# VectorE instead of GpSimd for the affine part of the residual and for the low weight parts at a layer's end

## The chip, the cores and the metric

The kernel runs on one core of a Trainium2 chip. The metric is the device time of one execution in microseconds (us). A core has a matrix engine (TensorE, PE in the profile; PEld is its weight load), VectorE (DVE), ScalarE (ACT), GpSimd (POOL) and SyncE (SP), whose queue issues the DMA transfers here. Each engine takes its instructions in the order in which the program lists them; engines wait for each other through semaphores.

## The reference, cut to what matters

One transformer block over 256 tokens of width 2048, in float32: a gated feed-forward network, a mixer (differential attention beside a gated delta rule) and a second feed-forward network. Each ends with a residual and a layer norm, and scale, shift and gate come from a vector `c`:

```python
ada = (jax.nn.silu(c) @ w_ada[l] + b_ada[l]).reshape(B, N_SUB, 3, D_MODEL)
shift, scale, gate = ada[:, :, 0, None], ada[:, :, 1, None], ada[:, :, 2, None]
y = swiglu_ffn(x * (1.0 + scale[:, 0]) + shift[:, 0], w_ffn_in[l, 0], w_ffn_out[l, 0])
x = layer_norm(DEEPNORM_ALPHA * x + 0.5 * gate[:, 0] * y, ln_g[l, 0], ln_b[l, 0])
y = hybrid_mixer(x * (1.0 + scale[:, 1]) + shift[:, 1], ...)
x = layer_norm(DEEPNORM_ALPHA * x + gate[:, 1] * y, ln_g[l, 1], ln_b[l, 1])
y = swiglu_ffn(x * (1.0 + scale[:, 2]) + shift[:, 2], w_ffn_in[l, 1], w_ffn_out[l, 1])
x = layer_norm(DEEPNORM_ALPHA * x + 0.5 * gate[:, 2] * y, ln_g[l, 2], ln_b[l, 2])
```

`layer_norm` multiplies the normed row by `ln_g` and adds `ln_b`: the affine part.

## The kernel before

**Products in three parts.** Every float32 matrix is split into a high part `hi` (a rounded copy) and a low part `lo` (what is left), and a product is three matmuls: high by high, low by high, high by low. A weight chunk of 128x1024 goes through four hands: SyncE loads it into one of six `raw` buffers, ScalarE writes `hi`, another engine subtracts and writes `lo` (four buffers each), and TensorE uses both in 24 matmuls of 256 columns or 12 of 512. A raw buffer is loaded anew when its `lo` is done; a `hi` buffer is written anew when TensorE is through with it. Which engine writes `lo` is decided in `_split`:

```python
eng = self.P if self.pool_lo and i % self.pool_lo == 0 else self.V
eng.tensor_tensor(lo, raw, hi.bitcast(F32), ALU.subtract)
```

`k.V`, `k.A` and `k.P` stand for VectorE, ScalarE and GpSimd. `pool_lo` is 1 or 2 in parts of the first layer's beginning, and 1 again at the ends of the first two layers, from `_Next.step` at stage 0 to `_Next.rest`.

**The order.** The kernel is written as Python generators ("threads") that a small planner steps while it writes TensorE's program. `k.t` is planned time; a thread that yields 8.0 is taken up again 8 planned us later, and what it then issues is put at that place of its engine's queue. So the planned times fix the order of each queue, and the chip decides the real times.

**The gate vectors.** `_Ada` loads `w_gate` chunks (`ar`, two buffers) and lets VectorE add them up: two instructions per chunk into `acc` (128x512), eight chunks for each quarter of a gate. Then ScalarE and VectorE split `acc` into `acchi` and `acclo`, and two matmuls with a matrix of ones (`aps`) sum over partitions. They stand in TensorE's queue between weight matmuls.

**The residual.** A layer's input after its norm is stored without the affine part (`xd`). `_load_x` reads it back while the next layer computes: into two tiles `x` (one per 128 tokens), then for each quarter of 512 columns the rows `ln_g` and `ln_b`, spread over 128 partitions, into `rowg` and `rowb` (one buffer each), and `x = x * rowg + rowb` for both tiles: 16 instructions in a layer, on GpSimd. This happens in the second layer (the mixer, while its output gates are multiplied, `gth`, `mf`, `mgl`) and in the third (the second feed-forward network, while `hid` is computed). The result is needed by the layer's output blocks, later.

**The layer end.** `_y_blocks` computes four output blocks of 512 columns; the last is cut into halves (`tail`), so that residual (`res`, `x`), statistics (`st`, `mv`, `rs`) and norm of one half run beside the matmuls of the next. Meanwhile weights of the next layer are loaded and split. TensorE then transposes the normed rows (`lnt`) and starts the next layer (`pre`).

Of the kernel before, what the change touches and what calls it, by code (L numbers as in the profile page):

```python
# [12 lines left out]
ALU = mybir.AluOpType  # L13
# [43 lines left out]
class _Thread:  # L57
# [6 lines left out]
    def step(self):  # L64
        k = self.k
        k.chain = k.t
        try:
            lat = next(self.gen)
            self.ready = k.t + max(0.0, lat) if lat is not None else k.t + MARGIN * (k.chain - k.t) + 0.3
        except StopIteration:  # L70
            self.done = True
            k.threads.remove(self)
# [186 lines left out]
def _products(k, ps, w, kt0, nkt, acts, first, last):  # L259

    nb = len(acts)
    hv, lv = [x.rearrange("p (k b m) -> p k b m", k=nkt, b=nb) for x in w]
    for j in range(nkt):
        for b in range(nb):
            acts[b].need(k, kt0 + j)
            ah, al = acts[b]
            k.mm3(ps[:, b, :], (hv[:, j, b, :], lv[:, j, b, :]),
                  (ah[:, kt0 + j, :], al[:, kt0 + j, :]),
                  start=(first and j == 0 and b == 0),
                  stop=(last and j == nkt - 1))  # L270
            k.pump()
# [214 lines left out]
def _new_h(k):  # L486
    u = k.uid()
    h = _H([k.pp.tile([128, KT, S], F32R, tag=f"h_{x}", name=f"h_{x}{u}") for x in ("hi", "lo")])
    h.ready = 0
    return h  # L490


def _h_tile(k, pool, h, f, src, A, B):

    nc = k.nc
    hf = pool.tile([128, S], F32, tag="hf", name=f"hf{k.uid()}", bufs=3)
    k.V.tensor_scalar(hf, src, A, B, ALU.mult, ALU.add)
    k.A.activation(h[0][:, f, :], hf, AF.Copy)
    k.P.tensor_tensor(h[1][:, f, :], hf, h[0][:, f, :].bitcast(F32), ALU.subtract)
# [45 lines left out]
class _Next:  # L545
# [5 lines left out]
    def step(self, stage, ada, ln):  # L551
        k = self.k
        if stage == 0:
            k.pool_lo = 1
            self.A = None
        elif stage == 1:
            ln.root(0)
        elif stage == 2:
            ln.factors(0)
        else:  # L560
            ln.norm(0, 0)
            ln.norm(0, 1)
            ln.root(1)
            return self.rest(ln)
        if self.A is None and (ada.thread.done or stage == 2):
            k.wait(lambda: ada.thread.done)
            self.A, self.B = self.prep(ada)

    def rest(self, ln):
        k, A, B = self.k, self.A, self.B  # L570
        h = _new_h(k)
        x, lnp = k.x, k.lnp
        k.xd = k.drp.tile([128, 2, D], F32, tag="xd", name=f"xd{self.idx}")

        def turn(ps, g, t):
            for j in range(2):
                f = 2 * g + j
                k.tr(ps[:, j, t * 128:(t + 1) * 128], x[t][:, f * 128:(f + 1) * 128])

        def bank(g):  # L580
            ps = k.pss.tile([128, 2, 256], F32, tag="sm", name=f"lnt{k.uid()}")
            turn(ps, g, 0)
            return ps

        ln.norm(0, 2)
        ln.norm(0, 3)
        pss = [bank(g) for g in range(3)]
        ln.factors(1)
        ln.norm(1, 0)
        k.pool_lo = 0  # L590
        def run():
            for g in range(8):
                ps = pss.pop(0)
                turn(ps, g, 1)
                for i in range(2):
                    f = 2 * g + i
                    _h_tile(k, lnp, h, f, ps[:, i, :], A[:, f:f + 1], B[:, f:f + 1])
                if g in (0, 2, 4):
                    ln.norm(1, 1 + g // 2)
                h.ready = 2 * g + 2  # L600
                h.when[2 * g] = h.when[2 * g + 1] = k.chain
                yield 0.0
                if g < 5:
                    pss.append(bank(g + 3))
            for t in range(2):
                k.nc.sync.dma_start(k.xd[:, t, :], x[t])

        th = k.spawn(run())
        th.step()
        acts = [h, h]  # L610
        pre = [k.bank([128, 2, S], "pre") for _ in range(2)]
        for c in range(4):
            for ps in pre:
                _products(k, ps, k.weights(), 4 * c, 4, acts, c == 0, c == 3)
        k.wait(lambda: th.done)
        return h, pre
# [46 lines left out]
def _load_x(k, a, pool, rows, tags, idx, delay, pace):  # L663

    nc = k.nc
    k.x = None
    yield delay
    x = [pool.tile([128, D], F32, tag=tags[t], name=f"x{k.uid()}") for t in range(2)]
    for q in range(4):
        for t in range(2):  # L670
            sl = slice(q * 512, (q + 1) * 512)
            nc.sync.dma_start(x[t][:, sl], k.xd[:, t, sl])
            k.load()
        yield pace
    for q in range(4 if idx is not None else 0):
        sl = slice(q * 512, (q + 1) * 512)
        g, b = [rows.tile([128, 512], F32, tag=n, name=f"{n}{k.uid()}", bufs=1) for n in ("rowg", "rowb")]
        nc.sync.dma_start(g, a["ln_g"][idx:idx + 1, sl].to_broadcast([128, 512]))
        nc.sync.dma_start(b, a["ln_b"][idx:idx + 1, sl].to_broadcast([128, 512]))
        yield 8.0  # L680
        for t in range(2):
            k.P.tensor_tensor(x[t][:, sl], x[t][:, sl], g, ALU.mult)
            k.P.tensor_tensor(x[t][:, sl], x[t][:, sl], b, ALU.add)
    k.x = x


# [73 lines left out]
def _ffn(k, a, h, sub, items, interval, start, pre, finish, tail):  # L760
# [4 lines left out]
    with ExitStack() as fs:  # L765
        k.hp = hp = fs.enter_context(tc.tile_pool(name=f"hid{sub}", bufs=1))
        for half, size in enumerate(SIZES[sub]):
            hid = _H([{}, {}])
            hid.ready = size
            j0 = 0  # L770
            if half == 0:

                def side():
                    k.pss = k.pss or k.ctx.enter_context(tc.tile_pool(name="pss", bufs=4, space=PSUM))
                    ada = _Ada(k, a, fs.enter_context(tc.tile_pool(name=f"ada{sub}", bufs=1)), items, interval)
                    k.lnp = fs.enter_context(tc.tile_pool(name=f"ln{sub}", bufs=1))
                    k.spawn(_load_x(k, a, k.lnp, k.lnp, ("x0", "x1"), *((1, 40.0, X_PACE) if sub else (None, 0.0, 3.0))))
                    return ada

                if start is not None:  # L780
                    j0 = size
                    ada = start(h, hid, side)
                    k.spawn(_rel_bias(k, a))
                    k.spawn(_lambda(k, a))
                    k.spawn(k.consts())
                else:
                    j0 = len(pre)
                    for j in range(j0):
                        _ffn_hid(k, pre[j], hid, j, back=j0 - j)
                    ada = side()  # L790
            for j in range(j0, size):
                ps = _wstat(k, 4, acts)
                _ffn_hid(k, ps, hid, j)
            res = _y_blocks(k, size // 2, hid, ada, sub, half == 0, ln if half else None, finish, tail)
# [103 lines left out]
def _delta_pair(k, g, kq2, v2, nz, yb, before, stage):  # L898
# [166 lines left out]
    for h in range(2):  # L1065
        k.mm(pz[:, reg(h)], U[:, 2 * h, 0, :], vn[:, 2 * h, :])
    z = tl("z", (128, 2, 128))
    k.A.activation(z, rest(pz[:, 0:256]), AF.Copy)
    yield

# [6 lines left out]
    for h in range(2):  # L1077
        k.mm(pS[:, reg(2 + h)], NQ[:, 2 * h, 1, :], z[:, h, :])
    St = tl("St", (128, 2, 128))
    k.V.tensor_copy(St, rest(pS[:, 0:256]))  # L1080
    for h in range(2):
        out(2 * h, pS[:, reg(2 + h)])
    oNv = oN.rearrange("p (h t) j -> p h t j", t=2)
    k.V.tensor_copy(oNv[:, :, 0, :], rest(pS[:, 256:512]))
    stage[0] = 4 * g + 2
    yield
# [619 lines left out]
```

## Time and profile before

| what | value |
|---|---|
| median of 3 runs | 2416.9 us (2414.76 to 2419.35) |
| the profiled execution's own time | 2417.43 us |
| its span, first to last instruction | 2415.6 us |
| outside the span | 1.8 us |
| mean granted TensorE clock | 0.984 of 2.4 GHz |
| PE busy | 2331.5 us (97%) |
| DVE busy | 1708.3 us (71%) |
| ACT busy | 1036.6 us (43%) |
| POOL busy | 323.1 us (13%) |

All times inside the execution count from the span's start. The layers end near 800 us and near 1637 us. A timeline row gives start, duration, engine, line, operation, output and inputs; "x2" merges two like instructions that follow each other, and the bracket names the idle time before it and what ended it.

### The profile page before, as it was taken

To read this page: it belongs to the slowest core of one execution; us is meant where nothing else is said; L and a number is where in the kernel's file an instruction comes from. 1 tells how busy PE (TensorE), PEld (TensorE's weight loads), DVE (VectorE), ACT (ScalarE), POOL (GpSimd) and SP (SyncE) were. 2 spreads that over 40 slices of the span, in tenths; PEclk is the share of its full clock that TensorE was granted. 3 is DMA by queue.
4 is the path that set the end of the run, shared out by engine and by line. 5 is a ranking of instruction groups with operands and counts; after the bars stand their busy time and mean duration, and the time that the engine had idled before them with its cause. 6 is when DMAs were issued, how large, how long until landed. Compare 5 with 4: busy or idle time off the path is not lost.

```text
span 2415.6 us, 42349 instructions
## 1 busy us (share of the span) xinstructions
PE 2331.5 (97%) x16989; PEld 2214.6 (92%) x16989; DVE 1708.3 (71%) x2538; ACT 1036.6 (43%) x1420; POOL 323.1 (13%) x218
## 2 busy tenths in 40 slices
PE   6999999999999899999999999999999999999997
PEld 6999997889998879998999999988999989999987
DVE  4767888787765687869887887876787555444456
ACT  4434444444444444444444344435434434444432
POOL 5884000000002210000000300022040000000001
PEclk8999999999999999999999999999999999999999
DMA  9997878898875565544547888876888555555553
GB/s 363 333 329 289 296 248 275 317 336 301 300 262 191 183 206 193 168 166 153 168 160 262 299 308 291 290 261 214 300 311 261 188 192 192 183 183 183 186 191 106
DMA packets 166381, 582.06 MB, mean 241 GB/s; under 512 B 19820, under 2 KB 22812, under 8 KB 165416
## 3 DMA queue, kind: packets, MB, share of 16 engines
q1 hardware_dynamic: 166184, 579.36, 68.9%
q8 instruction: 133, 2.18, 0.4%
q14 instruction: 64, 0.52, 0.1%
HBM read 572.98 MB, written 7.88 MB: 240 GB/s over the span
## 4 chain that ended last, share of the span: by engine, by line
PE 87%; DVE 7%; issue 2%; ACT 1%; DMA 1%; POOL 1%; DVEq 0%; SPq 0%; ACTq 0%; POOLq 0%
PE mm L147 15%; PE mm L148 15%; PE mm L149 15%; PE mx L149 8%; PE mx L147 8%; PE mx L148 8%; PE mms L148 4%; PE mms L147 4%; PE mms L149 4%; DVE lo L88 2%; DVE acc L88 1%; PE UY L153 1%; DVE x L88 1%; ACT hi L88 1%; PE pre L148 1%
## 5 line engine op out<-in xcount | busy, mean ns | idle before, releaser
L88 ACT ACTIVATE hi<-raw 128x1024 fp32r<-128x1024 f32 x769 | 811.9, 1059 | 995.9 <-PE mm L148 413.4
L88 DVE TENSOR_TENSOR lo<-raw,hi 128x1024 fp32r<-128x1024 f32 x690 | 855.2, 1245 | 524.6 <-ACT hi L88 516.8
L147 PE MATMUL mm<-h_hi,hi 128*128 128x256 f32 x3072 | 878.1, 286 | 0.0
L149 PE MATMUL mm<-h_hi,lo 128*128 128x256 f32 x3072 | 868.0, 283 | 3.6 <-DVE lo L88 3.6
L148 PE MATMUL mm<-h_lo,hi 128*128 128x256 f32 x3072 | 869.6, 283 | 0.0
L149 PEld LDWEIGHTS mm<-h_hi,lo 128*128 128x128 f32 x3072 | 583.3, 190 | 4.3 <-DVE lo L88 4.3
L147 PEld LDWEIGHTS mm<-h_hi,hi 128*128 128x128 f32 x3072 | 581.6, 189 | 1.9 <-issue 1.6
L148 PEld LDWEIGHTS mm<-h_lo,hi 128*128 128x128 f32 x3072 | 581.6, 189 | 1.0 <-issue 0.6
L88 POOL TENSOR_TENSOR lo<-raw,hi 128x1024 fp32r<-128x1024 f32 x79 | 189.9, 2412 | 793.4 <-ACT hi L88 793.4
L147 PE MATMUL mx<-hi,hid 128*128 128x512 f32 (+1 forms) x772 | 285.3, 370 | 1.4 <-ACT hi L88 1.4
L148 PE MATMUL mx<-lo,hid 128*128 128x512 f32 (+1 forms) x772 | 285.3, 370 | 0.8 <-DVE lo L88 0.8
L149 PE MATMUL mx<-hi,hid 128*128 128x512 f32 (+1 forms) x772 | 285.1, 369 | 0.0
L147 PE MATMUL mms<-h_hi,hi 128*128 128x256 f32 x896 | 256.2, 286 | 9.9 <-ACT hi L88 5.7
L148 PE MATMUL mms<-h_lo,hi 128*128 128x256 f32 x896 | 255.4, 285 | 3.7 <-POOL h_lo L88 3.7
L149 PE MATMUL mms<-h_hi,lo 128*128 128x256 f32 x896 | 254.3, 284 | 1.6 <-POOL lo L88 1.6
L147 PEld LDWEIGHTS mms<-h_hi,hi 128*128 128x128 f32 x896 | 170.5, 190 | 10.6 <-ACT hi L88 5.8
L148 PEld LDWEIGHTS mms<-h_lo,hi 128*128 128x128 f32 x896 | 171.3, 191 | 4.3 <-POOL h_lo L88 4.2
L149 PEld LDWEIGHTS mms<-h_hi,lo 128*128 128x128 f32 x896 | 172.1, 192 | 1.9 <-POOL lo L88 1.9
L147 PEld LDWEIGHTS mx<-hi,hid 128*128 128x128 f32 x772 | 145.5, 189 | 26.7 <-ACT hi L88 1.9
L148 PEld LDWEIGHTS mx<-lo,hid 128*128 128x128 f32 x772 | 145.5, 188 | 25.9 <-DVE lo L88 1.4
L149 PEld LDWEIGHTS mx<-hi,hid 128*128 128x128 f32 x772 | 145.5, 188 | 24.4
L88 DVE SCALAR_TENSOR_TENSOR acc<-ar,cs,acc 128x512 f32<-128x512 f32 x180 | 147.7, 821 | 6.3 <-DMA ar<-in_w_gate_dram 2.9
(295 smaller groups left out, 2436.7 us busy)
## 6 DMA issues: line engine op xcount, KB each, us to landing
raw<-in_w_ffn_in_dram SPq DMA_DIRECT2D x240, 512.0 KB, 4.4
raw<-in_w_ffn_out_dram SPq DMA_DIRECT2D x176, 512.0 KB, 4.1
raw<-in_w_first_dram SPq DMA_DIRECT2D x112, 512.0 KB, 5.1
ar<-in_w_gate_dram SPq DMA_DIRECT2D x96, 512.0 KB, 4.9
ar<-in_w_ada_dram SPq DMA_DIRECT2D x96, 512.0 KB, 5.4
sar<-in_w_ada_dram SPq DMA_DIRECT2D x64, 512.0 KB, 4.7
raw<-in_w_gab_dram SPq DMA_DIRECT2D x64, 512.0 KB, 4.7
raw<-in_w_kq_dram SPq DMA_DIRECT2D x32, 512.0 KB, 3.2
```

What stands on the lines that cost most here:

```text
L88: return f(*args, **kw)
L147: mm(ps, lhsT=lhs[0], rhs=rhs[0], start=start, stop=False, skip_group_check=True)
L148: mm(ps, lhsT=lhs[0], rhs=rhs[1], start=False, stop=False, skip_group_check=True)
L149: mm(ps, lhsT=lhs[1], rhs=rhs[0], start=False, stop=stop, skip_group_check=True)
L153: self.nc.tensor.matmul(ps, lhsT=lhsT, rhs=rhs, start=start, stop=stop, skip_group_check=True)
```

## The change

`pool_lo` is no longer set at the layers' ends, so the seven low parts of each end are VectorE's. The 32 affine instructions are VectorE's too, and each has its own step: a quarter was one wait of 8 planned us and four instructions at once; now it is 4 planned us and then four instructions with 2 planned us ahead of each, 12 in all.

```diff
     def step(self, stage, ada, ln):
         k = self.k
         if stage == 0:
-            k.pool_lo = 1
             self.A = None
...
         ln.factors(1)
         ln.norm(1, 0)
-        k.pool_lo = 0
+
         def run():
...
-        yield 8.0
+        yield 4.0
         for t in range(2):
-            k.P.tensor_tensor(x[t][:, sl], x[t][:, sl], g, ALU.mult)
-            k.P.tensor_tensor(x[t][:, sl], x[t][:, sl], b, ALU.add)
+            for v, op in ((g, ALU.mult), (b, ALU.add)):
+                yield 2.0
+                k.V.tensor_tensor(x[t][:, sl], x[t][:, sl], v, op)
```

The first place is SyncE's queue in the mixer, where the second quarter's rows are loaded. `raw` is a weight load, `ar` a load of the gate's weights, and the bracket names the semaphores that the issue waits for. Before:

```order
L173 DMA raw_15164<-in_w_br_dram 128x1024 [waits DMAHW2_49,DVE_49]
L382 DMA ar_15171<-in_w_gate_dram 128x1024 [waits DMAHW3_49,DVE_49]
L678 DMA rowg_15195<-in_ln_g_dram 128x512 [waits DMAHW5_49,DMAHW4_49,Pool_49]
L679 DMA rowb_15196<-in_ln_b_dram 128x512 [waits DMAHW6_49,Pool_49]
L173 DMA raw_15206<-in_w_gab_dram 128x1024 [waits DVE_49]
L173 DMA raw_15239<-in_w_gab_dram 128x1024 [waits DMAHW7_49,DVE_49]
```

And of the change:

```order
L173 DMA raw_15199<-in_w_gab_dram 128x1024 [waits DMAHW4_49,DVE_49]
L173 DMA raw_15234<-in_w_gab_dram 128x1024 [waits DMAHW5_49,DVE_49]
L677 DMA rowg_15258<-in_ln_g_dram 128x512 [waits DMAHW6_49]
L678 DMA rowb_15259<-in_ln_b_dram 128x512 [waits DMAHW7_49,DVE_49]
L382 DMA ar_15267<-in_w_gate_dram 128x1024 [waits DMAHW0_49,DVE_49]
L173 DMA raw_15273<-in_w_gab_dram 128x1024 [waits DMAHW1_49,DVE_49]
```

The row loads stand two weight loads later, and the semaphore of GpSimd is gone: a row buffer is free when VectorE's last reader is done.

The second place is VectorE's queue at the same stretch, from the first affine instruction on (- before, + the change).

```order
-L88 TENSOR_TENSOR lo_15203<-raw_14997,hi_15202 128x1024
-L88 TENSOR_TENSOR lo_15236<-raw_15030,hi_15235 128x1024
+L88 TENSOR_TENSOR x_14661<-x_14661,rowg_15080 128x512
+L88 TENSOR_TENSOR lo_15196<-raw_14997,hi_15195 128x1024
+L88 TENSOR_TENSOR x_14661<-x_14661,rowb_15081 128x512
+L88 TENSOR_TENSOR x_14662<-x_14662,rowg_15080 128x512
+L88 TENSOR_TENSOR lo_15231<-raw_15030,hi_15230 128x1024
+L88 TENSOR_TENSOR x_14662<-x_14662,rowb_15081 128x512
 L88 SCALAR_TENSOR_TENSOR acc_14963<-ar_15116,cs,acc_14963 128x512 x2
 L88 TENSOR_TENSOR lo_15270<-raw_15060,hi_15269 128x1024
```

Affine instructions now stand between the low parts. Eight of the mixer's 16 stand ahead of the last addition into the second quarter's `acc`, and all 16 ahead of that of the third; in the third layer four stand ahead of it. In TensorE's queue the `aps` matmuls of these quarters stand later by 9 and by 99 matmuls in the mixer, and by 6 in the third layer.

The third place is VectorE's queue at the end of the first layer; `res_8516` begins the first half of the last output block.

```order
 L88 TENSOR_TENSOR x_2813<-x_2813,res_8325 128x512
 L88 BN_STATS st_90<-x_2813 128x6 x2
+L88 TENSOR_TENSOR lo_8349<-raw_8210,hi_8348 128x1024
+L88 TENSOR_TENSOR lo_8379<-raw_8228,hi_8378 128x1024
+L88 TENSOR_TENSOR lo_8409<-raw_8246,hi_8408 128x1024
+L88 TENSOR_TENSOR lo_8439<-raw_8264,hi_8438 128x1024
+L88 TENSOR_TENSOR lo_8469<-raw_8282,hi_8468 128x1024
+L88 TENSOR_TENSOR lo_8499<-raw_8312,hi_8498 128x1024
 L88 SCALAR_TENSOR_TENSOR res_8516<-mx_8304,gate_2786 128x256
 L88 TENSOR_TENSOR x_2812<-x_2812,res_8516 128x256
```

Six of the seven low parts now stand right ahead of the last block's residual (the seventh stands ahead of the block before); GpSimd's queue has none of them.

## Rows read from the trace of the kernel before

**Rows 1.** The page: busy time of each engine, and the costliest group of ScalarE.

```profile
PE 2331.5 (97%) x16989; PEld 2214.6 (92%) x16989; DVE 1708.3 (71%) x2538; ACT 1036.6 (43%) x1420; POOL 323.1 (13%) x218
...
L88 ACT ACTIVATE hi<-raw 128x1024 fp32r<-128x1024 f32 x769 | 811.9, 1059 | 995.9 <-PE mm L148 413.4
```

**Rows 2.** Busy time by stretch: length, then PE, PEld, DVE, ACT, POOL, clock, DMA.

```profile
1300.00:1350.00 50.00, 50.00 (x417) 49.92 (x417) 39.41 (x47) 20.24 (x25) 0.00 (x0) 1.00 0.91 329
1350.00:1400.00 50.00, 46.99 (x376) 46.37 (x376) 46.90 (x40) 19.65 (x23) 27.57 (x16) 0.97 0.82 273
...
1700.00:1750.00 50.00, 50.00 (x417) 49.92 (x416) 35.05 (x42) 22.19 (x28) 0.00 (x0) 1.00 0.89 303
1750.00:1800.00 50.00, 46.63 (x372) 46.01 (x372) 44.48 (x40) 19.74 (x26) 26.38 (x16) 0.97 0.88 306
```

**Rows 3.** Timeline of PE at three `aps` places, two in the mixer.

```profile
1384.25 0.28 PE L149 MATMUL mm<-h_hi,lo 128*128 128x256 f32 x1
1386.97 0.50 PE L153 MATMUL aps<-acchi,ones 128*128 128x512 f32 x1 [2.44 <-ACT acchi L88]
...
1388.64 0.41 PE L147 MATMUL mm<-h_hi,hi 128*128 128x256 f32 x1
...
1419.54 0.28 PE L149 MATMUL mm<-ybh,lo 128*128 128x256 f32 x1
...
1422.01 0.28 PE L147 MATMUL mm<-yah,hi 128*128 128x256 f32 x1
...
1772.74 0.28 PE L149 MATMUL mm<-h_hi,lo 128*128 128x256 f32 x1
...
1777.48 0.42 PE L147 MATMUL mm<-h_hi,hi 128*128 128x256 f32 x1
```

**Rows 4.** Groups of GpSimd: the multiplications by the row.

```profile
L88 POOL TENSOR_TENSOR x<-x,rowg 128x512 f32<-128x512 f32 x16 | 28.2, 1759 | 185.6 <-DMA rowg<-in_ln_g_dram 185.6
```

**Rows 5.** Timeline of VectorE around the mixer's affine part.

```profile
1342.08 1.22 DVE L88 TENSOR_TENSOR lo<-raw,hi 128x1024 fp32r<-128x1024 f32 x1
...
1355.37 1.84 DVE L88 TENSOR_TENSOR lo<-raw,hi 128x1024 fp32r<-128x1024 f32 x1 [0.39 <-ACT hi L88]
...
1383.51 2.75 DVE L88 SCALAR_TENSOR_TENSOR acc<-ar,cs,acc 128x512 f32<-128x512 f32 x2 [0.61 <-DMA ar<-in_w_gate_dram]
...
1393.49 4.15 DVE L88 SCALAR_TENSOR_TENSOR acc<-ar,cs,acc 128x512 f32<-128x512 f32 x3
...
1402.41 1.53 DVE L88 SCALAR_TENSOR_TENSOR acc<-ar,cs,acc 128x512 f32<-128x512 f32 x2
```

**Rows 6.** SyncE's queue in the mixer: waits of 1340 to 1400, then its timeline.

```profile
SPq L678 <- POOL x L88: 9.0, 3, 5.3
...
1361.08 1.30 SPq L678 DMA_DIRECT2D rowg<-in_ln_g_dram  x1
...
1366.60 0.33 SPq L173 DMA_DIRECT2D raw<-in_w_gab_dram  x1
1372.49 0.33 SPq L678 DMA_DIRECT2D rowg<-in_ln_g_dram  x1
...
1375.04 0.42 SPq L382 DMA_DIRECT2D ar<-in_w_gate_dram  x1
```

**Rows 7.** Timeline of GpSimd: the first instruction after a row load.

```profile
1367.26 1.53 POOL L88 TENSOR_TENSOR x<-x,rowg 128x512 f32<-128x512 f32 x1 [5.49 <-DMA rowg<-in_ln_g_dram]
```

**Rows 8.** Timeline at both layer ends: VectorE's residual and GpSimd's last low part.

```profile
788.68 2.40 POOL L88 TENSOR_TENSOR lo<-raw,hi 128x1024 fp32r<-128x1024 f32 x1 [0.48 <-ACT hi L88]
...
789.39 1.97 DVE L88 TENSOR_TENSOR x<-x,res 128x256 f32<-128x256 f32 x1
...
792.18 0.42 DVE L88 TENSOR_TENSOR x<-x,res 128x256 f32<-128x256 f32 x1
...
1625.96 1.90 DVE L88 SCALAR_TENSOR_TENSOR x<-x,res 128x256 f32<-128x256 f32 x1
```

**Rows 9.** Timeline of VectorE: one instruction on 128x512, both inputs in SBUF.

```profile
771.04 0.69 DVE L88 TENSOR_TENSOR x<-x,res 128x512 f32<-128x512 f32 x1
```

## The prediction

> **What bounds the kernel now.** I began with the page: TensorE is busy 97% of the span [rows 1], so only places where it stops, or runs at its lower clock, are worth anything. The table by stretch finds them where GpSimd does the affine part. In 1300 to 1350 us TensorE gets through 417 matmuls, 0.12 us each; in 1350 to 1400, through 376 with 27.6 us of GpSimd beside it; in the third layer it is 417 and then 372 [rows 2]. Between 1400 and 1750 GpSimd has nothing of the kind.
>
> TensorE's timeline says where it stopped. After the matmul of 1384.25 the next is an `aps`, which came at 1386.97 because it waited for `acchi`; weight matmuls go on at 1388.64. The same happens at 1419.54 to 1422.01 and at 1772.74 to 1777.48 [rows 3]. TensorE does not lack weights there: an `aps` stands in its queue for a sum that VectorE has not finished, and all weight matmuls queue behind it. So what bounds these two stretches is how late VectorE is when TensorE reaches an `aps`.
>
> Why VectorE is late is in its timeline. A `lo` takes 1.22 us and a pair of `acc` additions 1.53 when GpSimd is idle; with GpSimd at work a `lo` takes up to 1.84 and more, and three `acc` additions 4.15 [rows 5]. I read every VectorE row from the first (1355.37) to the last (1393.49) of these, 12 stretched rows, against its plain duration: 14.1 us too much in the mixer, 10.6 of it by the nine rows up to 1383.51. The third layer, read the same way, has 13.7. SyncE is held up too: it issues a weight load at 1366.60 and its next load, `rowg`, only at 1372.49, because GpSimd still reads the one row buffer; three such waits are 9.0 us [rows 6], with weight and gate loads queued behind.
>
> **The change part by part.** *Affine part, the price.* No affine instruction ran on VectorE. The nearest row is the same operation on the same shape, `x<-x,res`, 0.69 us [rows 9]: 16 cost 11.0 us in each layer. A lower price has no row; the upper end is 1.76, GpSimd's own mean for it [rows 4]. I take 0.69, since operation, engine, shape and memory are the same. So VectorE's load falls by 14.1 - 11.0 = 3.1 us in the mixer and by 13.7 - 11.0 = 2.7 in the third layer: a small relief, because VectorE pays for the work either way.
>
> A rule bears on this. The stretched rows show VectorE losing 14.1 us to 16 GpSimd instructions. The Trainium skill, "SBUF — State Buffer", section "Who interferes with whom", says that a VectorE instruction with two SBUF inputs and a GpSimd instruction that reads SBUF exclude each other for a whole instruction. By it 16 instructions of 1.76 us could hold VectorE for up to 28 us, and the relief would be up to 17 us; the trace agrees that one waits for the other, and goes by 14.1.
>
> *Affine part, where it lands.* What counts is VectorE's lateness at each `aps`. At the mixer's first stopping place eight affine instructions stand ahead of the last addition: 8 x 0.69 = 5.5 us in place of 10.6, so `acc` is ready 5.1 us sooner; TensorE gets there 9 matmuls (1.1 us) later. The `aps` was late by 1386.97 - 1384.37 (one matmul after 1384.25) = 2.6 us, and `acclo` adds about another 1.2. 6.2 us cover that with 2.4 to spare. At the second place VectorE's queue from the first affine instruction to the last addition sums to about 59 us (20 `lo` at a pitch of 1.14, 16 affine, 24 additions, three sets of `gth`, `mf`, `mgl`), from 1358 on: 1417. TensorE comes 99 matmuls (11.9 us) later, less the 4.7 us that it no longer loses: near 1427. In the third layer four affine instructions (2.8 us) stand ahead of the sum. So I expect all three stops to go. What they cost: 417 - 376 = 41 matmuls, less two for the `aps` (each as long as two), is 39 x 0.12 = 4.7 us, clock included; 2.47 us less 0.58 for the `aps` and a matmul is 1.9; and 43 x 0.12 = 5.2 in the third layer. Together 11.8.
>
> *Cover.* VectorE is busy 39.4 of 50 us in the mixer without GpSimd [rows 2]; with 11.0 it is 50.4 of 50, full. About 3 us more go in waits for `mgh`. The lag of some 3.4 us is hidden by the lead of the weights: a `hi` buffer comes free three chunks ahead of its use, 3 x 24 x 0.12 = 8.6 us, less 1.06 for `hi` [rows 1] and 1.22 for `lo` leaves 6.3. Without that lead it would be TensorE's loss. The third layer has 35.1 + 11.0 = 46.1 of 50.
>
> *Row loads.* VectorE now waits for a row itself, with `lo` queued behind, and TensorE behind those. A row issued at 1361.08 was used by GpSimd at 1367.26 [rows 6, 7]: 6.2 us, my upper value. VectorE's own work between a row's issue and its first use sums to 9.3, 9.6, 9.9 and 7.0 us in the mixer and 5.6, 6.3, 4.8 and 4.8 in the third layer. So only there may it wait, 0.6 + 1.4 + 1.4 = 3.4 us, against 3.9 us of idle time and the 6.3 us of lead. Nothing to 3.4 us; I set aside 1.5 for this and for stops that I don't see. SyncE's issues no longer wait for GpSimd; that is worth nothing by itself once the `aps` are on time.
>
> *Layer ends.* The last low part held the residual: `x<-x,res` took 1.97 us from 789.39 where its like takes 0.42, and 1.90 from 1625.96 [rows 8]. VectorE then works without a break until the norm, so TensorE's wait for `lnt` follows it. Now `lo` stands ahead of `res`: 788.68 + 1.22 + 0.43 + 0.42 = 790.75 where it was 791.36, 0.6 us sooner; twice, 1.2. The bounds are nothing (a later wait takes it up) and 1.5 each (the whole stretch). The other low parts fall into a stretch where VectorE waits for `mx`, and cost nothing.
>
> **Sum.** 11.8 + 1.2 - 1.5 = 11.5 us off the profiled 2417.43: 2405.9. That execution was 0.5 above the median of the runs, so I say **2405.5 us**.
>
> **The rivals.** *All stops go* (the forecast): 10 to 13.5 us.
>
> *VectorE becomes the bound.* For it: 50.4 of 50 us, with nothing left for a wait. Then lateness is conserved, and TensorE gets only what VectorE's load falls by: 3.1 + 2.7 + 1.2 = 7.0 us, 2410. With 0.85 us for an affine instruction in its queue it is 14.1 - 13.6 + 13.7 - 13.6 + 1.2 = 1.8: 2415, no change. Against it: the `aps` stand later, and the lead holds 6.3 us. It decides from 39.4 + 3 + 16 x 0.85 = 56 of 50 us on, where the lead is used up.
>
> The Trainium skill, "Perfetto Trace Analysis", section "Optimizing Scalar/DVE Operations", sides with this rival: where VectorE is saturated, moving work to ScalarE or even GpSimd may make sense, though it warns that GpSimd shares a port with VectorE. By its first half this change would go the wrong way.
>
> *Rows come late* (the other side). The gate load of 1375.04 was used at 1383.51 [rows 5, 6], 8.5 us. If rows took that, the waits would be 1.5 us in the mixer and 12.5 in the third layer, 9.9 of them covered there: the gain shrinks to about 9. At 10.3 us and more for every row, covers, idle time and lead are used up, about 13 us are lost, and the kernel is slower than before: 2418 and up. Against it: no row load shows more than 6.2, and the rows move the same bytes over a longer time.
>
> **How the numbers follow.** Forecast 0.62; VectorE the bound with 5 to 9 us gained 0.14, with less than that 0.12; rows late 0.06 with no change and 0.06 slower. A measurement of this kernel tells about 0.2% (4.8 us) from no change. Faster 0.76, same 0.18, slower 0.06. The forecast's own range is 2403.4 to 2406.9; the range over cases goes from 2402.5 (full stretch at the layer ends, no new wait) to 2412 (VectorE the bound, most of the way).
>
> **What would show it.** Right: 410 or more matmuls where there were 376 and 372, no `aps` preceded by more than 0.5 us of idle time in these stretches, plain `lo` rows of 1.22, affine rows of 0.69, SyncE's waits for `rowg` under 1 us each. Wrong: VectorE rows that wait for `rowg`, `aps` still waiting for `acchi`, or weight matmuls that wait for `lo`, which today hardly happens.

## The result and the profile after

The kernel after takes 2404.5 us (median of 5 runs, 2402.6 to 2405.6) where the kernel before takes 2416.9: a ratio of 0.9948, with a 95% interval of 0.9937 to 0.9959. 2405.5 was forecast. The profiled execution has a span of 2403.7 us, 11.9 less than that of before.

The page's busy times, which answer to [rows 1]: GpSimd has 46 instructions fewer and VectorE 46 more, and VectorE's busy time is the same to 2 us, because it no longer takes longer beside GpSimd.

```profile
PE 2327.8 (97%) x16989; PEld 2210.9 (92%) x16989; DVE 1710.1 (71%) x2584; ACT 1036.3 (43%) x1420; POOL 234.0 (10%) x172
```

The table by stretch (length, then busy time of PE, PEld, DVE, ACT and POOL, clock, DMA), which answers to [rows 2]:

```profile
1300.00:1350.00 50.00, 50.00 (x418) 49.92 (x416) 39.24 (x45) 21.31 (x25) 0.00 (x0) 1.00 0.92 329
1350.00:1400.00 50.00, 50.00 (x417) 49.92 (x416) 45.01 (x58) 22.18 (x26) 0.00 (x0) 1.00 0.92 300
1400.00:1450.00 50.00, 50.00 (x417) 49.92 (x416) 43.39 (x54) 20.72 (x26) 0.00 (x0) 1.00 0.88 306
...
1750.00:1800.00 50.00, 50.00 (x417) 49.91 (x416) 39.23 (x52) 21.64 (x27) 0.00 (x0) 1.00 0.90 327
```

TensorE gets through 417 matmuls where there were 376 and 372, at the full clock where it was 0.97. VectorE has 45.0 and 43.4 of 50 us in the mixer, not a full 50: its 16 affine instructions lie between 1359 and 1414.

The timelines of VectorE and TensorE at the mixer's two stopping places, which answer to [rows 3]:

```profile
1384.18 0.68 DVE L88 TENSOR_TENSOR acclo<-acc,acchi 128x512 fp32r<-128x512 f32 x1
1386.94 0.39 PE L153 MATMUL aps<-acchi,ones 128*128 128x512 f32 x1
...
1425.55 0.68 DVE L88 TENSOR_TENSOR acclo<-acc,acchi 128x512 fp32r<-128x512 f32 x1
1427.71 0.39 PE L153 MATMUL aps<-acchi,ones 128*128 128x512 f32 x1
```

No idle time stands in brackets behind the `aps` any more. The second operand of the sum is ready 2.1 us ahead at the first place (1386.94 - 1384.18 - 0.68) and 1.5 us ahead at the second. There VectorE's last addition and ScalarE's `acchi` stand ahead of `acclo`:

```profile
1419.24 1.53 DVE L88 SCALAR_TENSOR_TENSOR acc<-ar,cs,acc 128x512 f32<-128x512 f32 x2
1424.27 0.61 ACT L88 ACTIVATE acchi<-acc 128x512 fp32r<-128x512 f32 x1
```

VectorE's timeline in the mixer, which answers to [rows 5]:

```profile
1358.00 1.53 DVE L88 SCALAR_TENSOR_TENSOR acc<-ar,cs,acc 128x512 f32<-128x512 f32 x2
1359.45 0.69 DVE L88 TENSOR_TENSOR x<-x,rowg 128x512 f32<-128x512 f32 x1
1360.06 1.22 DVE L88 TENSOR_TENSOR lo<-raw,hi 128x1024 fp32r<-128x1024 f32 x1
1361.19 0.68 DVE L88 TENSOR_TENSOR x<-x,rowb 128x512 f32<-128x512 f32 x1
```

Its group of multiplications by the row (busy time, mean ns of one, then the idle time ahead of them), which answers to [rows 4, 9]:

```profile
L88 DVE TENSOR_TENSOR x<-x,rowg 128x512 f32<-128x512 f32 x16 | 11.0, 686 | 5.7 <-DMA rowg<-in_ln_g_dram 5.7
```

SyncE's wait for a `rowg` buffer, from the view of waits between 1350 and 1420 us (total, times, longest), which answers to the first row of [rows 6]:

```profile
SPq L677 <- DVE x L88: 1.0, 1, 1.0
```

Affine instructions take 0.69 us among plain `lo` of 1.22 and pairs of `acc` of 1.53, and SyncE hardly waits. The group's idle time shows a new wait: VectorE waits 5.7 us for rows. The timeline has it in two places, both in the third layer. SyncE issued the row of the second wait at 1787.00, 9.7 us before its use:

```profile
1779.17 0.69 DVE L88 TENSOR_TENSOR x<-x,rowg 128x512 f32<-128x512 f32 x1 [2.01 <-DMA rowg<-in_ln_g_dram]
...
1787.00 0.42 SPq L677 DMA_DIRECT2D rowg<-in_ln_g_dram  x1
...
1796.72 0.69 DVE L88 TENSOR_TENSOR x<-x,rowg 128x512 f32<-128x512 f32 x1 [3.68 <-DMA rowg<-in_ln_g_dram]
```

The first layer end on VectorE, which answers to [rows 8]: the last `lo` holds `res` back a little, and `x` takes 0.42 us where it took 1.97.

```profile
787.75 1.22 DVE L88 TENSOR_TENSOR lo<-raw,hi 128x1024 fp32r<-128x1024 f32 x1 [1.66 <-ACT hi L88]
788.89 0.41 DVE L88 SCALAR_TENSOR_TENSOR res<-mx,gate 128x256 f32<-128x256 f32 x1
789.34 0.42 DVE L88 TENSOR_TENSOR x<-x,res 128x256 f32<-128x256 f32 x1
```

**Where the time came from.** Single runs of one kernel differ by several us, so the sum of the time says little about a part worth 1 us. Marks that every kernel has in the same order say more. Six were taken; these are their rows in the timeline of after (the first residual of layer 1, the start of the mixer, the mixer's first gate, ScalarE's `rs<-eps` ahead of the second layer end, the first `hf` of that end, and a residual inside the third layer, behind its affine part):

```profile
407.73 0.68 DVE L88 SCALAR_TENSOR_TENSOR res<-mx,gate 128x512 f32<-128x512 f32 x1
828.67 0.15 DVE L88 TENSOR_SCALAR dnw<-dnw 128x1 f32<-128x1 f32 x1
1339.28 0.58 ACT L88 ACTIVATE gate<-aps 128x512 f32<-128x512 f32 x1
1600.67 0.20 ACT L88 ACTIVATE rs<-eps 128x1 f32<-128x1 f32 x1
1629.37 0.99 DVE L88 TENSOR_SCALAR hf<-lnt,affA,affB 128x256 f32<-128x256 f32 x2 [0.79 <-PE lnt L158]
1985.94 0.68 DVE L88 SCALAR_TENSOR_TENSOR res<-mx,gate 128x512 f32<-128x512 f32 x1
```

In the trace of before the same marks start at 408.57, 830.28, 1337.78, 1606.37, 1635.88 and 1997.85. The table has how much shorter each stretch between two marks is than in before (us; minus is longer); "rest" is the difference of the spans less these five.

```
                 end 1   mixer,      mixer,    end 2   third   rest   span
                         1st half    affine            layer
after            +0.77    -3.11      +7.20     +0.81   +5.40  +0.83  2403.7
after_again      +0.75    -1.11      +7.19     +0.82   +5.39  -0.04  2402.6
ends_only        +0.75    +0.39      -2.40     +0.74   +1.48  +0.74  2413.9
affine_only      +0.02    -2.70      +7.19     +0.07   +5.40  +1.02  2404.6
spread_pool      +0.77    -0.37      -1.76     +0.68   +5.40  +0.78  2410.1
wide_pool        +0.77    -1.10      -1.35     +0.68   +5.23  -1.03  2412.4
lump_dve         +0.77    -0.43      +6.23     +0.82   +5.40  +0.51  2402.3
no_affine        +0.77    -1.01      +7.22     +0.81   +5.41  +0.20  2402.2
half_more_dve    +0.77    -0.67      +4.34     +1.48   +4.30  +0.48  2404.9
twice_dve        +0.74    +0.29      +2.07     +1.41   +1.88  +1.11  2408.1
rows2_before     -0.00    -3.16      -1.25     -0.01   -1.75  +0.17  2421.6
rows2_after      +0.81    -1.30      +6.88     +0.81   +5.40  -0.70  2403.7
rows_late        +0.75    -1.08     -12.55     +0.81  -12.37  -0.36  2440.4
```

The reader should compare within a column. The affine stretches give 7.2 and 5.4 us in both profiles of after, in affine_only and in no_affine; the layer ends give some 0.8 each where their low parts are on VectorE. The mixer's first half, in which all these kernels have the same instructions, differs by up to 3.5 us from run to run. With GpSimd at work the affine stretches vary too: before, ends_only and rows2_before issue the same instructions there, and differ by up to 2.4 us in the mixer and 3.2 in the third layer. Each row is one profile, so the gains of 7.20 and 5.40 hold against this profile of before. In half_more_dve and twice_dve the second end shows 0.6 us more than in after; why stays open.

### The profile page after: what moved, and what is told of

Read it like the earlier page. It is cut to its first block, busy times and chain, and to the rows that moved or that the text cites. A ratio compares the mean times of both kernels' runs of the same rounds, so it can differ in the third digit from the quotient of the medians.

```text
span 2403.7 us, 42329 instructions
## 1 busy us (share of the span) xinstructions
PE 2327.8 (97%) x16989; PEld 2210.9 (92%) x16989; DVE 1710.1 (71%) x2584; ACT 1036.3 (43%) x1420; POOL 234.0 (10%) x172
## 4 chain that ended last, share of the span: by engine, by line
PE 89%; DVE 6%; issue 2%; ACT 1%; POOL 1%; DMA 0%; SPq 0%; DVEq 0%; ACTq 0%; POOLq 0%
PE mm L147 16%; PE mm L148 16%; PE mm L149 16%; PE mx L147 8%; PE mx L149 8%; PE mx L148 8%; PE mms L148 4%; PE mms L149 4%; PE mms L147 4%; DVE lo L88 2%; ACT hi L88 1%; PE UY L153 1%; DVE acc L88 1%; DVE x L88 1%; PE pre L148 1%
## 5 line engine op out<-in xcount | busy, mean ns | idle before, releaser
L147 PEld LDWEIGHTS mms<-h_hi,hi 128*128 128x128 f32 x896 | 170.6, 190 | 11.9 <-ACT hi L88 7.3
L88 POOL TENSOR_TENSOR lo<-raw,hi 128x1024 fp32r<-128x1024 f32 x65 | 155.2, 2399 | 36.7 <-ACT hi L88 36.2
L88 DVE SCALAR_TENSOR_TENSOR acc<-ar,cs,acc 128x512 f32<-128x512 f32 x180 | 134.8, 749 | 8.3 <-DMA ar<-in_w_gate_dram 4.9
```

Source lines behind the costliest of these rows:

```text
L88: return f(*args, **kw)
L147: mm(ps, lhsT=lhs[0], rhs=rhs[0], start=start, stop=False, skip_group_check=True)
```

## The experiments

**The two halves.** Each half was applied to the kernel before alone. Each ratio from here on is to runs of the kernel before taken beside that kernel (medians 2417.1 to 2417.8 us).

```diff
 ends_only
-            k.pool_lo = 1
...
-        k.pool_lo = 0
 affine_only
+            for v, op in ((g, ALU.mult), (b, ALU.add)):
+                yield 2.0
+                k.V.tensor_tensor(x[t][:, sl], x[t][:, sl], v, op)
```

> Only the seven low parts at each layer end go to VectorE; the affine part stays on GpSimd in lumps. By the prediction's term for the layer ends: 0.6 us each, 1.2 us off the time before, about 2415.7. By what the trace of after shows from the last residual to the first transpose (9.29 and 9.88 us where it was 10.84 and 11.50): 1.6 us each, 3.2 us off, about 2413.7. If what is gained at the first end is lost again before the mixer's affine part, as the counts of matmuls in after suggest (1.4 us behind at 1350), only the second end's gain stays: 2414.5 to 2415.5.

Measured: 2416.3 us, ratio 0.9996 (0.9987 to 1.0005). By the marks each end gives 0.75 us, 1.5 together, the size that the prediction gave (0.6 each). The time can't show that much: the affine stretches, which this kernel doesn't touch, lost 2.4 and gave 1.5 in the same execution.

> Only the affine part goes to VectorE, spread as in the change; the low parts at the layer ends stay on GpSimd. By the prediction: 11.8 - 1.5 = 10.3 us off the time before, 2406.6. By the counts of matmuls in after (60 in the mixer, 45 in the third layer, 0.12 us each): 12.6 us off, 2404.3. The rival that VectorE becomes the bound would leave 5.8 us, 2411.

Measured: 2406.4 us, ratio 0.9951 (0.9939 to 0.9964). The columns of the affine part are those of after, 7.19 and 5.40, and the layer ends give nothing. The two halves add up.

**Engine or order.** The change gives the affine part another engine and other pauses. These runs hold one of the two fixed. The engine brings its place in the program along: in lump_dve the planner puts the mixer's next three `aps` 87, 120 and 66 matmuls later than in before, while in spread_pool and wide_pool they stand where they stood.

```diff
 spread_pool
-                k.V.tensor_tensor(x[t][:, sl], x[t][:, sl], v, op)
+                k.P.tensor_tensor(x[t][:, sl], x[t][:, sl], v, op)
 lump_dve
-        yield 4.0
+        yield 8.0
...
-                yield 2.0
 wide_pool (on spread_pool)
-        yield 4.0
+        yield 12.0
```

> The change with its spreading (4 + 4 x 2.0 us per quarter) and its layer ends, but the affine instructions stay on GpSimd. Engine theory (VectorE loses some 14 us per layer to GpSimd's instructions wherever they stand): GpSimd still stretches lo and acc rows, some aps still wait for acchi, and only part of the gain comes: 2408 to 2414. Order theory (it is the wider spreading that lets VectorE be in time, whichever engine does it): 2404.5 within 1.5 us, with 410 or more matmuls per 50 us in both stretches.

Measured: 2413.8 us, ratio 0.9986 (0.9977 to 0.9995). Neither theory holds everywhere, as the stretches of this kernel and the rows of TensorE's timeline show:

```profile
1350.00:1400.00 50.00, 48.81 (x403) 48.24 (x402) 47.11 (x42) 21.00 (x25) 21.93 (x12) 1.00 0.84 272
1400.00:1450.00 50.00, 45.10 (x357) 44.14 (x357) 41.23 (x48) 17.81 (x22) 5.39 (x4) 0.97 0.87 301
...
1750.00:1800.00 50.00, 50.00 (x417) 49.91 (x416) 43.39 (x43) 22.38 (x30) 20.41 (x12) 1.00 0.88 313
...
1384.01 0.50 PE L153 MATMUL aps<-acclo,ones 128*128 128x512 f32 x1 [0.37 <-DVE acclo L88]
...
1410.24 0.58 PE L149 MATMUL mm<-h_hi,lo 128*128 128x256 f32 x1 [2.83 <-DVE lo L88]
```

In the mixer the loss moves, from 1350 to 1400 into 1400 to 1450, and the stretch is 1.8 us longer than in before, so nothing is gained: there the engine is what counts. The stops also change their kind. The first `aps` waits 0.37 us where it waited 3.0, the second waits as before, and 4.4 of TensorE's 6.1 us of idle time are weight matmuls that wait for a `lo`, the longest 2.83 us. VectorE beside GpSimd is now late with the low parts. In the third layer the spacing alone is enough: 417 matmuls with GpSimd at work for 20.4 us, and the full 5.40 us.

> The change with the affine part on VectorE, but its four instructions of a quarter in one lump after 8.0 planned us, as before the change. Engine theory: a lump is 4 x 0.69 = 2.8 us of VectorE, which the weights' lead of 6.3 us covers; at most one aps waits: 2404.5 to 2407. Order theory: the stops come back, since the sums stand behind the lumps as before: 2411 or more.

Measured: 2404.5 us, ratio 0.9944 (0.9932 to 0.9957). On VectorE the lumps cost 1.0 us in the mixer, where the third `aps` waits 0.71 us for `acclo`, and nothing in the third layer. So in the mixer it is the engine, with the later places, that brings the gain, and the spreading adds at most that 1 us; in the third layer either edit alone is enough.

> The affine part stays on GpSimd, but a quarter takes 12 + 4 x 2.0 = 20 planned us instead of 8 (before) or 12 (the run with the spreading alone); the layer ends are those of after. If what counts is how much of GpSimd's work falls into the same few microseconds of VectorE (its 14 us of loss per layer now lie over some 85 us, within VectorE's idle time and the weights' lead), the stops go in the mixer too, although GpSimd does the work: 2404.5 to 2408. If any aps that is reached with GpSimd at work waits, the mixer still loses 7 us as in the run with the spreading alone: 2411 to 2414.

Measured: 2412.2 us, ratio 0.9978 (0.9969 to 0.9988). With 20 planned us for a quarter the third layer keeps 5.23 us and the mixer still gains nothing (-1.35). TensorE's timeline in the mixer has the stops of before again, each an `aps`:

```profile
1386.48 0.50 PE L153 MATMUL aps<-acchi,ones 128*128 128x512 f32 x1 [0.55 <-ACT acchi L88]
1388.64 0.67 PE L153 MATMUL aps<-acclo,ones 128*128 128x512 f32 x1 [1.66 <-DVE acclo L88]
...
1421.85 0.49 PE L153 MATMUL aps<-acchi,ones 128*128 128x512 f32 x1 [1.08 <-ACT acchi L88]
1422.92 0.80 PE L153 MATMUL aps<-acclo,ones 128*128 128x512 f32 x1 [0.58 <-DVE acclo L88]
```

What GpSimd takes from VectorE does not depend on the spacing either. These are VectorE's groups by shape between 1350 and 1420 us (busy, then mean ns of one), of spread_pool:

```profile
L88 DVE SCALAR_TENSOR_TENSOR acc<-ar,cs,acc 128x512 f32<-128x512 f32 x27 | 29.9, 1109 | 4.2 <-DMA ar<-in_w_gate_dram 3.6
L88 DVE TENSOR_TENSOR lo<-raw,hi 128x1024 fp32r<-128x1024 f32 x21 | 28.0, 1351 | 2.5 <-ACT hi L88 2.5
```

and the same two groups of after:

```profile
L88 DVE TENSOR_TENSOR lo<-raw,hi 128x1024 fp32r<-128x1024 f32 x23 | 27.9, 1221 | 3.5 <-ACT hi L88 2.4 <-DMA raw<-in_w_gab_dram 0.5 <-DMA rowb<-in_ln_b_dram 0.5
L88 DVE SCALAR_TENSOR_TENSOR acc<-ar,cs,acc 128x512 f32<-128x512 f32 x26 | 19.5, 749 | 2.1 <-DMA ar<-in_w_gate_dram 1.6
```

The first two of before, over the same stretch, are

```profile
L88 DVE TENSOR_TENSOR lo<-raw,hi 128x1024 fp32r<-128x1024 f32 x22 | 31.3, 1442 | 1.4 <-ACT hi L88 1.4
L88 DVE SCALAR_TENSOR_TENSOR acc<-ar,cs,acc 128x512 f32<-128x512 f32 x27 | 27.2, 1006 | 2.9 <-DMA ar<-in_w_gate_dram 2.4
```

For spread_pool 27 x (1.109 - 0.749) = 9.7 us and 21 x (1.351 - 1.221) = 2.7; with VectorE's other shapes, read the same way, 13.4 us. Before has 13.9, ends_only 15.6, wide_pool 14.6 (10.5, and 4.1 from 1420 to 1460), the kernel after 0.0.

**What is left of the cost, and where VectorE becomes the bound.** no_affine drops the affine part. The other two double instructions on VectorE.

```diff
 no_affine
-                k.V.tensor_tensor(x[t][:, sl], x[t][:, sl], v, op)
 twice_dve (half_more_dve: for the multiplications alone)
+                k.V.tensor_tensor(y, x[t][:, sl], v, op)
                 k.V.tensor_tensor(x[t][:, sl], x[t][:, sl], v, op)
```

> The kernel after without the affine part in the mixer and the third layer: x is used as normalized, without g and b, and the rows are not loaded; the planned pauses stay. It shows what the affine part still costs. My theory: TensorE loses nothing to it any more, so 2403.5 to 2405.5. If VectorE's 11.0 us in each layer still cost something (later sums, later gates), 2 to 4 us less.

Measured: 2405.0 us, ratio 0.9946 (0.9932 to 0.9959). The affine stretches are 7.22 and 5.41 us shorter than in before, those of after 7.20 and 5.40: on VectorE the affine part costs nothing. This run also settles the cause of the stops. TensorE's order here has every `aps` at the same place as before, and none of the mixer's or the third layer's stops: what made them late was the affine part on GpSimd, not their place. The row loads, which this run drops too, are not the cause: after has them, and its VectorE rows take their plain time.

> The kernel after with each of the 16 multiplications of the affine part issued twice, the first time into a scratch tile: 5.5 us more of VectorE in each of the two layers. By the prediction's threshold of 56 of 50 us: 39.4 + 3 + 16.5 = 58.9 in the mixer, 2.9 us lost, and 51.6 in the third layer, nothing lost: 2407.4. By the run with every instruction twice, which lost 5.1 us in the mixer and 3.5 in the third layer (the threshold then stands at about 16.9 and 18.5 us of affine work): nothing lost in either, 2404 to 2405.5.

Measured: 2406.7 us, ratio 0.9958 (0.9945 to 0.9970). The mixer loses 7.20 - 4.34 = 2.9 us, the third layer 1.1. TensorE's stops in the mixer are of both kinds, 1.23 us for a `lo` and 1.10 us of the third `aps` for `acclo`.

> The kernel after, with every affine instruction on VectorE issued twice, the first time into a scratch tile: 32 more VectorE instructions of 0.69 us, 11.0 us more in each of the two layers, with the same result. By the prediction's threshold (VectorE becomes the bound from 56 of 50 us on): 39.4 + 3 + 22 = 64.4 of 50 in the mixer and 35.1 + 22 = 57.1 in the third layer, so 8.4 + 1.1 us are lost, about 2414. By the rows of after (45.0 and 43.4 of 50 us busy in the mixer, 39.2 and 39.6 in the third layer, since the 16 instructions lie over more than 50 us): VectorE comes only some 5 us late in the mixer, within the weights' lead of 6.3 us, and 0 to 3 us are lost: 2404.5 to 2407.5.

Measured: 2412.9 us, ratio 0.9977 (0.9967 to 0.9987). The mixer loses 5.1 us, the third layer 3.5: 8.6 together. TensorE's timeline shows another kind of stop, a weight matmul that waits for its low part:

```profile
1405.68 0.39 PE L149 MATMUL mm<-h_hi,lo 128*128 128x256 f32 x1 [0.98 <-DVE lo L88]
1409.47 0.39 PE L147 MATMUL mm<-h_hi,hi 128*128 128x256 f32 x1 [0.89 <-ACT hi L88]
1410.73 0.39 PE L149 MATMUL mm<-h_hi,lo 128*128 128x256 f32 x1 [0.76 <-DVE lo L88]
...
1791.82 0.39 PE L149 MATMUL mm<-h_hi,lo 128*128 128x256 f32 x1 [1.46 <-DVE lo L88]
```

This is the rival "VectorE becomes the bound", as it looks when it is true: the weights' lead is used up. In after it is not.

**The row loads.**

```diff
 rows2_before, rows2_after
-        g, b = [rows.tile([128, 512], F32, tag=n, name=f"{n}{k.uid()}", bufs=1) for n in ("rowg", "rowb")]
+        g, b = [rows.tile([128, 512], F32, tag=n, name=f"{n}{k.uid()}", bufs=2) for n in ("rowg", "rowb")]
 rows_late
-        yield 4.0
         for t in range(2):
             for v, op in ((g, ALU.mult), (b, ALU.add)):
-                yield 2.0
                 k.V.tensor_tensor(x[t][:, sl], x[t][:, sl], v, op)
+                yield 2.0
+        yield 4.0
```

> The kernel before with two buffers for each row in place of one, so that SyncE no longer waits for GpSimd's reads (9.0 us in three waits in the mixer) before it issues the next rows and the weight and gate loads behind them. My theory: GpSimd still runs beside VectorE and the aps still come late, so nothing changes: 2415.5 to 2418. Rival: the held-up loads were part of the loss; then up to the 5 to 7 us of the stops come back, 2410 to 2412.

Measured: 2420.5 us, ratio 1.0011 (1.0002 to 1.0020), above the range that was expected. In the mixer SyncE's waits for GpSimd at the rows, 9.0 us for `rowg` [rows 6] and 2.5 for `rowb`, are gone; in the whole execution, where before has 23.0, one is left:

```profile
SPq L679 <- POOL x L88: 0.3, 1, 0.3
```

and nothing is gained: the affine stretches are 1.25 and 1.75 us longer than in before, about as much as they differ in ends_only, which leaves them alone (2.4 longer and 1.5 shorter). The waits on SyncE were no part of the loss.

> The kernel after with two buffers for each row. VectorE's two waits for a row in the third layer (2.01 and 3.68 us) shrink or go, since the rows can be issued while the quarter ahead is still being worked on. My theory: these waits were hidden from TensorE, so the time stays, 2403.5 to 2405.5. Rival (the waits were paid for somewhere): 3 to 5 us less, 2400 to 2401.5.

Measured: 2405.3 us, ratio 0.9945 (0.9932 to 0.9957). The waits for rows only shrink from 5.7 to 4.9 us, so this run does not take them away as it was meant to. That they were hidden is shown by the third layer's 5.40 us with and without the affine part.

> The kernel after with the pause of 4.0 planned us behind the four instructions of a quarter instead of ahead of them, so that VectorE's first instruction stands in its queue right behind the row's issue: the cover of 5 to 10 us is gone. It tests the prediction's rival on late rows, by its own rule (VectorE bound from 56 of 50 us on). If a row takes 6.2 us, four waits of some 5 us per layer: 53.4 + 20 in the mixer and 46.1 + 20 in the third layer, 17 + 10 us lost, 2431. If it takes 3 us: 53.4 + 12 and 46.1 + 12, 9 + 2 us lost, 2416. If VectorE's waits were hidden whatever their size, 2404.5.

Measured: 2440.2 us, ratio 1.0095 (1.0078 to 1.0112), 35.7 us more than after. The view of waits has eight for a row and, on TensorE, nine for a `lo` (after has two, 3.4 us):

```profile
DVE x L88 <- DMA rowg<-in_ln_g_dram: 48.8, 8, 7.4
...
PE mm L149 <- DVE lo L88: 20.7, 9, 5.4
```

VectorE waits 48.8 / 8 = 6.1 us each time; from its issue to its use a row takes 4.8 to 7.0 us, 5.8 in the mean, near the prediction's 6.2. The expectation's 2431 for that case was 9 us too low: 19.8 us are lost in the mixer and 17.8 in the third layer. The clock was left out of it. In the table by stretch TensorE is idle for 23.6 us between 1350 and 1500 and between 1750 and 1850, near the 27 that were expected, but the granted clock (a mean over the row) falls as well, as two of these rows show:

```profile
1350.00:1400.00 50.00, 41.21 (x313) 39.28 (x311) 31.64 (x41) 14.27 (x17) 0.00 (x0) 0.95 0.66 217
...
1750.00:1800.00 50.00, 44.44 (x341) 43.52 (x340) 32.67 (x42) 18.27 (x24) 0.00 (x0) 0.93 0.77 256
```

In the second, 5.6 us are idle, and 417 - 341 = 76 matmuls or 9.1 us are missing; a clock of 0.93 over 50 us is worth the other 3.5. The timeline shows one of the waits and the matmul that pays for it:

```profile
1825.72 0.69 DVE L88 TENSOR_TENSOR x<-x,rowg 128x512 f32<-128x512 f32 x1 [6.70 <-DMA rowg<-in_ln_g_dram]
...
1829.05 0.58 PE L149 MATMUL mm<-h_hi,lo 128*128 128x256 f32 x1 [5.43 <-DVE lo L88]
```

**Chance.** The kernel after was profiled a second time.

> The kernel after once more, unchanged, to see how much of the difference from stage to stage is chance. My theory: in the first half of the mixer (830 to 1338 us) the same instructions take up to some 2 us more or less from one execution to the next, so this profile differs there from the first one of after, and within 0.3 us in the stretches of the affine part and the layer ends; the time is 2403 to 2406.

Measured: 2404.3 us, ratio 0.9948 (0.9936 to 0.9961). Four columns agree with the first profile of after within 0.02 us; the mixer's first half differs by 2.0 us and the rest by 0.9.

## Why the prediction was right, point by point

*What bounds it.* Right. TensorE stopped at `aps` whose sums came late because VectorE ran beside GpSimd; without GpSimd (after, no_affine) no `aps` of the mixer or the third layer stops, with it the mixer's do in wide_pool. In spread_pool VectorE is late too, but TensorE waits mostly for its low parts.

*Price.* Right: 0.69 us for an affine instruction, 11.0 for 16 in each layer. VectorE's loss under GpSimd was read as 14.1 and 13.7; by shapes it is 13.9 and 13.5. On the rule of the Trainium skill ("SBUF — State Buffer", "Who interferes with whom"), by which up to 28 us could be lost: every run with GpSimd in the mixer's affine part lost 13 to 16 us, about half of that bound. This is within the rule and no test of it: no run tells what sets the half.

*Where it lands.* The stops went, but the terms were too small: 4.7 + 1.9 = 6.6 in the mixer measured 7.20, and 5.2 measured 5.40. I had taken two matmuls off each count for the `aps`, which run in any case. Without that the counts give it exactly: (417 - 376) + (417 - 398) = 60 matmuls, 7.2 us, and 417 - 372 = 45, 5.4 us. The 398 are those of before in the next stretch:

```profile
1400.00:1450.00 50.00, 48.48 (x398) 47.72 (x398) 43.08 (x53) 20.97 (x25) 0.00 (x0) 1.00 0.89 317
```

At the second place the margin was mis-sized. TensorE came at 1427.7, as forecast, but the last addition ended at 1420.8 and not at 1417, and the split of the sum, which the forecast left out there, took 5.5 us more, to the end of `acclo`: 1.5 us of margin in place of 10. With VectorE's queue as it stands, the sum would have come 11.9 - 1.5 = 10.4 us too late for the old place, so this stop went with the 99 matmuls by which the `aps` stands later.

*Cover.* The mechanism holds, and the figure roughly. The threshold of 56 of 50 us gave losses of 2.9 + 0 us for half_more_dve (measured 2.9 + 1.1) and 8.4 + 1.1 for twice_dve (5.1 + 3.5): the sums are near, the split between the layers is not. For rows_late it gave 27 us, near TensorE's 23.6 us of idle time; that a stop can also cost clock is not in it. VectorE was not full, though, since the 16 instructions lie over more than 50 us.

*Row loads.* The place was right (third layer alone), the size not: 5.7 us of waiting where at most 3.4 was expected. The upper value of 6.2 us for a row was too low: the two rows waited for took 6.6 and 9.7 us from issue to use. By the prediction's own list VectorE rows that wait for `rowg` were a sign of being wrong; they came, cost nothing, and used none of the reserve of 1.5 us.

*SyncE.* Right: worth nothing by itself (rows2_before).

*Layer ends.* 0.77 and 0.81 us where 0.6 was said, near enough; `lo` does stand ahead of `res` and gives part of the 1.5 back.

*The sum.* It came out right, partly by luck. The terms were 11.8 + 1.2 = 13.0 and measured 12.6 + 1.6 = 14.2, and the reserve of 1.5 us was not needed, so the forecast of 11.5 was 2.7 too small. What brought the profiled execution back to 11.9 is chance: its mixer's first half took 3.1 us more and the rest 0.8 less (the second profile has 1.1 and 0.0). The middle one of the thirteen profiles is 1.1 us longer there than that of before, so before was profiled in a quick execution of that half. By the marks the change itself is worth about 14 us against the profiled execution of before; the medians are 12.4 apart, and 13.3 in the runs beside after_again.

*The rivals.* VectorE as the bound begins somewhere between 11.0 us of affine work per layer (no loss) and 16.5 (2.9 and 1.1). The advice of the Trainium skill ("Perfetto Trace Analysis", "Optimizing Scalar/DVE Operations") to move work from a saturated VectorE to GpSimd would not have helped here: VectorE is not saturated in after (45.0 of 50 us), and 11.0 us of work moved to GpSimd take 14 from VectorE. Its warning that such a move might not help agrees with this; that a shared port is the reason no run here shows. Late rows are a real danger (rows_late: 35.7 us), which here the pause ahead of the instructions keeps away. The prediction's argument against them, that no row load shows more than 6.2 us, did not hold (9.7 in after).

**What stays open.** Why the mixer stops with GpSimd at work whatever the spacing, and the third layer does not, was not isolated. VectorE has more of its own work in the mixer (39.4 of 50 us against 35.1), which fits, as do the late low parts of spread_pool, but is only argued. With the affine part on VectorE the program also puts the mixer's next three `aps` 9, 99 and 30 matmuls later; neither VectorE's instructions with the `aps` left in place nor GpSimd's with the `aps` moved were tried, so how much of the 7.2 us the later places alone would bring, at the second stop above all, stays open. At the first place 1.1 us earlier would still have been in time (2.1 us to spare).

## What to carry to other kernels

Work on GpSimd can cost VectorE time: compare its own price on VectorE (here 11.0 us) with what VectorE's rows lose while GpSimd runs (13 to 16 us), and if VectorE keeps slack, try it there. Where a planner orders the program, as here, an instruction on VectorE is in its account and moves what depends on it (the `aps`); a slowdown by a neighbour is not. A load that VectorE waits for needs its pause ahead of the first use, and to judge parts worth a microsecond, compare marks from stage to stage, not the total time.

## What was not expected of the hardware

Sixteen GpSimd instructions took 13 to 16 us from VectorE in the mixer in all five kernels that have them there (rows2_before: 15.4), packed or spread, over 42 to 88 us. A stop of TensorE can cost more than its idle time: before, PE is idle for 3.0 of the 50 us from 1350 but 41 matmuls (4.9 us) are missing, with the granted clock at 0.97 [rows 2]; in rows_late, from 1750, 5.6 us are idle and 9.1 missing, at 0.93; in half_more_dve, in the stretch from 1400, 1.2 us idle are 12 matmuls (1.4 us), at the full clock. And the mixer's first half varied by 3.5 us over thirteen profiles of kernels that are the same there. The granted clock goes along: this stretch of after

```profile
1100.00:1150.00 50.00, 47.19 (x368) 46.16 (x367) 43.70 (x110) 20.86 (x37) 3.28 (x3) 0.93 0.48 163
```

has 368 matmuls at a clock of 0.93, and of ends_only

```profile
1100.00:1150.00 50.00, 47.08 (x389) 46.05 (x388) 45.89 (x113) 22.38 (x40) 3.57 (x3) 1.00 0.51 168
```

389 with the same busy time. What decides which of the two an execution gets stays open.
